# Gate tiles in pairs: sums of the seven products made in open PSUM banks, copied out by ScalarE

## The chip, the cores and the metric

The kernel runs on one core of a Trainium2 chip. A core has TensorE (PE, the matrix multiplier, with its weight loads PEld beside it), VectorE (DVE), ScalarE (ACT), GpSimd (POOL) and SyncE (SP, which issues nearly all DMA transfers here). Each engine has a queue of its own, worked off in order, and engines wait for one another through semaphores. PE writes its products into PSUM, eight banks of 128 x 512 float32 each, which DVE and ACT read; everything else lies in SBUF or in device memory. The metric is the time of one execution in microseconds (us) on the device.

## The reference

A decoder layer with two attention branches for one sequence of 2048 tokens, width 1024. One input projection gives the queries, keys and values of both branches, and the gates:

```python
xn = rms_norm(h, norm_gain[l])
proj = xn @ w_in[l]
sb_q, sb_k, sb_v, sw_q, sw_k, sw_v, sb_z, sw_z, g_sb, g_sw = jnp.split(proj, offsets, axis=-1)
...
y_sb = (o_sb * jax.nn.silu(sb_z)) @ w_branch_sb[l]
y_sw = (o_sw * jax.nn.silu(sw_z)) @ w_branch_swa[l]
merged = jax.nn.sigmoid(g_sb) * y_sb + jax.nn.sigmoid(g_sw) * y_sw
h = h + merged @ w_out[l]
```

The change concerns columns of this projection that become gates: `sb_z` and `sw_z` go through SiLU (a value times its sigmoid), `g_sb` and `g_sw` through a sigmoid.

## The kernel before

The tokens are cut into four groups of 512; groups 2 and 3 are worked on first, then 0 and 1. Columns of the projection are cut into tiles of 128. The normalized input is kept transposed as two parts, a rounded high part `xh[g]` and the rest `xl[g]`, and so are the weights (`wh`, `wl`); a product is three matmuls (high x high, high x low, low x high) for each of eight slices of 128 rows. A plain column tile (`col_tile`) is 24 matmuls of 128x512 and its gate is made by `gate` (L1339, L1341).

**Seven products in place of eight.** `gate_pairs` takes two column tiles c and d and the two groups ga and gb of a half at once, as a 2 x 2 block product: the weights are the blocks a11, a12 (tile c) and a21, a22 (tile d), the inputs b11, b21 (group ga) and b12, b22 (group gb), each block four slices deep. Strassen's scheme in Winograd's form makes the four results from seven products. It needs sums of weight blocks, s1 to s4, made for each pair by `pair_weights` (DVE makes the sums r1 to r4, ACT rounds them to high parts `sh`, DVE makes the low parts `sl`), and sums of input blocks, t1 to t4, made once for a call. It runs twice: for the last 16 gate tiles of the first half (eight pairs, 0 to 7), and for eight SiLU tiles of the second half (four pairs, 8 to 11). Pairs 1 to 6 and 8 to 11 are SiLU gates, pairs 0 and 7 are plain sigmoids.

**The work of a pair before.** `product(a, b)` (L1924 to L1932) takes the next of three bank tags g, z, t (two banks each, so six products may be in flight) and runs 12 matmuls, L1929 to L1931. The order is a11·b11, a12·b21, s2·t2, s4·b22, a22·t4, s1·t1, s3·t3. ACT copies the first out of PSUM (L1953); seven additions on DVE (`add`, L1935), each with one operand in PSUM, form the results; `gate_out` applies sigmoid (L1940, L1943) and for SiLU a multiplication (L1941), and sends the result out by DMA.

**Buffers.** The results and r1 to r4 come from the ring `tmp` of nine tiles of 128x512 (L1112), the s blocks from rings of four (`SB = 4`), the whole weights from rings of three, raw weights from two. A tile is given out in the program's order when an older one is released.

**What sets the order.** PE's order is the order of the program throughout (`manual_schedule`). DVE follows the program up to `ordered()` in the first pair of a call (`byhand.close` or `rest`); ACT follows it up to the call. Otherwise a planner lays out ACT, DVE and SP ahead of time: it simulates the engines, and gives each engine the earliest instruction of the program that is ready in that simulation. On the chip the engines then keep that order, ready or not. Around the calls: in pair 0, `put` (L1740, L1741) still fills t1 and t3; `along` runs squares of the next half's rows (L1892) on ACT in the first call and weight sums for the last projection on DVE in the second; in the last pair of the first call `between` prepares the next group.

Of the kernel before, what the change touches and what calls it, by code (L numbers as in the profile page):

```python
# [10 lines left out]
AF = mybir.ActivationFunctionType  # L11
ALU = mybir.AluOpType
# [37 lines left out]
def tile_kernel(ctx, tc, x, xt, meta, metat, gain, w_in, w_sb, w_sw, w_out, sinks, fgain,  # L50
# [16 lines left out]
    def ps(tag):  # L67
        return pp.tile([P, 512], F32, tag=tag, name="ps_" + tag, bufs={"g": 2, "z": 2, "t": 2, "o": 2}[tag])
# [102 lines left out]
    def drain(*gens):  # L171
        for _ in chain(*gens):
            pass
# [938 lines left out]
    def tmp(dt=F32, rows=P):  # L1112
        return tp.tile([rows, GT], dt, tag="tmp", name="tmp", bufs=9)
# [623 lines left out]
    HK = KT // 2  # L1737
# [114 lines left out]
    def pair_weights(c, d, pool, out, begin=False):  # L1852

        raws, whole = [], []
        for c0 in (c, d):
            raws.append(load(c0))
            whole.append(weights(c0, raw=raws[-1]))
            yield
        a11, a12, a21, a22 = (r[:, j:j + HK, :] for r in raws for j in (0, HK))
        r1, r2, r3, r4 = (tmp().rearrange("p (k c) -> p k c", k=HK) for _ in range(4))  # L1860
        s2, s1, s3, s4 = ([pool.tile([P, HK, P], F32R, tag="s" + i, name="s" + i, bufs=SB) for i in "hl"] for _ in range(4))
        V.tensor_tensor(r1, a21, a22, op=ALU.add)
        V.tensor_tensor(r2, r1, a11, op=ALU.subtract)
        if begin:
            A.copy(s2[0], r2)
            A.copy(s1[0], r1)
        V.tensor_tensor(r3, a11, a21, op=ALU.subtract)
        if begin:
            A.copy(s3[0], r3)
            V.tensor_tensor(s2[1], r2, f32(s2[0]), op=ALU.subtract)  # L1870
            yield
        V.tensor_tensor(r4, a12, r2, op=ALU.subtract)
        if begin:
            A.copy(s4[0], r4)
        for (h, l), r in ((s2, r2), (s1, r1), (s3, r3), (s4, r4)):
            if not begin:
                A.copy(h, r)
            if r is not r2 or not begin:
                V.tensor_tensor(l, r, f32(h), op=ALU.subtract)
        (h1, l1), (h2, l2) = whole  # L1880
        out.extend([(h1[:, :HK, :], l1[:, :HK, :]), (h1[:, HK:, :], l1[:, HK:, :]), (h2[:, HK:, :], l2[:, HK:, :]),
                    s1, s2, s3, s4])
# [34 lines left out]
    def gate_pairs(ga, gb, pairs, pool, sums_x, nxt, ordered, along, between):  # L1917

        t1, t2, t3, t4 = sums_x[:4]
        b11, b21 = ((xh[ga][:, j:j + HK, :], xl[ga][:, j:j + HK, :]) for j in (0, HK))  # L1920
        b22 = xh[gb][:, HK:, :], xl[gb][:, HK:, :]

        banks = iter(range(1 << 30))

        def product(a, b):
            acc = ps("gzt"[next(banks) % 3])
            (wh, wl), (h, l) = a, b
            for k in range(HK):
                T.matmul(acc, lhsT=wh[:, k, :], rhs=h[:, k, :], start=k == 0, stop=False)  # L1929
                T.matmul(acc, lhsT=wh[:, k, :], rhs=l[:, k, :], start=False, stop=False)  # L1930
                T.matmul(acc, lhsT=wl[:, k, :], rhs=h[:, k, :], start=False, stop=k == HK - 1)  # L1931
            return acc  # L1932

        def add(t, acc, u):
            V.tensor_tensor(t, acc, u, op=ALU.add)  # L1935

        def gate_out(dst, t, silu):
            if silu:
                e = tmp()
                A.activation(e, t, AF.Sigmoid)  # L1940
                V.tensor_tensor(t, t, e, op=ALU.mult)  # L1941
            else:
                A.activation(t, t, AF.Sigmoid)  # L1943
            DMA(dst, t)

        for n, ((_, cdst, csilu), (_, ddst, dsilu)) in enumerate(pairs):
            a11, a12, a22, s1, s2, s3, s4 = nxt
            end = n + 1 == len(pairs)
            if n and not end:
                nxt = []  # L1950
                drain(pair_weights(pairs[n + 1][0][0], pairs[n + 1][1][0], pool, nxt))
            p, u, v, w = (tmp() for _ in range(4))
            A.copy(p, product(a11, b11))  # L1953
            more = product(a12, b21)
            add(u, product(s2, t2), p)
            add(p, more, p)
            if not n:
                nxt = []
                ordered()
                drain(pair_weights(pairs[1][0][0], pairs[1][1][0], pool, nxt))  # L1960
            gate_out(cdst[ga], p, csilu)
            next(along, None)
            if end:
                between()
            p3 = product(s4, b22)
            p4 = product(a22, t4)
            p5 = product(s1, t1)
            add(v, p5, u)
            add(v, p3, v)
            gate_out(cdst[gb], v, csilu)  # L1970
            add(u, product(s3, t3), u)
            add(w, p5, u)
            gate_out(ddst[gb], w, dsilu)
            add(u, p4, u)
            gate_out(ddst[ga], u, dsilu)


    sbt = [lambda p=p, f=f: f(p) for f, p in ((sb_k, 0), (sb_k, 1), (sb_q, 0), (sb_v, 0), (sb_v, 1), (sb_q, 1),
# [174 lines left out]
    for half, groups in enumerate(halves):  # L2153
        gts = [lambda spec=spec: gate(*spec) for spec in specs[half]]
        if half == 1:
            with tc.tile_pool(name="fast1", bufs=1, side="left") as bp:
                byhand, hand = ExitStack(), ExitStack()
                byhand.enter_context(tc.manual_schedule(engines={mybir.EngineType.DVE}))
                hand.enter_context(tc.manual_schedule(engines={mybir.EngineType.Activation}))
                vsplit[0] = True  # L2160
                ts = [mk() for mk in sbt[:3]]
                *sums_x, late_lows, side = combined_anew(*groups, rs1, bp, short)
                pairs = list(zip(swz[::2], swz[1::2]))
                nxt = []
# [88 lines left out]
        if half == 0:  # L2253
            with tc.tile_pool(name="fast", bufs=1, side="left") as bp:
# [25 lines left out]
        else:  # L2280
# [95 lines left out]
```

## Time and profile before

| | |
|---|---|
| time, median of 3 runs | 2049.21 us (2048.4 to 2049.78) |
| span of the profiled execution, first to last instruction | 2045.8 us |
| its own time | not listed apart from the span; the median is 3.4 us above it |
| first call of `gate_pairs` | 580.4 to 733.9 us of the span |
| second call | 777.6 to 854.1 us |

The profile is one execution recorded by the hardware profiler. Its page gives the busy time of each engine, the chain of work that ended last, and groups of instructions by source line. The trace behind it answers further views: windows (busy time of each engine in a stretch), waits (who waited for whom), and a timeline, whose rows are start, duration, engine, source line, operation, output<-inputs, shapes and count; brackets hold the idle time ahead of an instruction and what ended it. Consecutive instructions of one kind may be merged in a row ("x3"). Matmuls overlap: a matmul's row is longer than the step from one to the next.

### The profile page before, as it was taken

Reading aid. Unit: us, or ns where it says so; the run is one execution under the profiler, and the core shown is the slowest. Engines: PE = TensorE matmul, PEld = TensorE weight load, DVE = VectorE, ACT = ScalarE, POOL = GpSimd, SP = SyncE. Lnnn points to the kernel's source line nnn. Section 1 sums busy time; section 2 is a strip of 40 time slices with the busy share of each in tenths; the row PEclk is TensorE's granted clock in tenths of the full one; section 3 lists DMA queues with packets and bytes.
Section 4 is the critical chain, followed back from the end, with each engine's and each line's share of the span. In section 5 each row is a group of like instructions: output and inputs, shape, how many; then the busy total and the mean of one; then the engine's idle time right before and its main releaser. Section 6 shows DMA issues by size and latency. Waiting matters only on the chain.

```text
span 2045.8 us, 31245 instructions
## 1 busy us (share of the span) xinstructions
PE 2031.7 (99%) x10375; PEld 1706.3 (83%) x10375; DVE 1649.3 (81%) x2708; ACT 1177.5 (58%) x2825; POOL 311.4 (15%) x642
## 2 busy tenths in 40 slices
PE   9999999999999999999999999999999999999998
PEld 7888888888888888888888888888888888887887
DVE  7898986877788789658887389999997788788788
ACT  6677775576755343358777366667766442335234
POOL 1233444431000000003333101000000003000000
PEclk9999999999999999999999999999999999999999
DMA  9855554865468669844344554344323779886942
GB/s 336 321 197 199 179 200 165 260 194 170 135 233 306 228 214 315 309 147 162 132 178 150 173 156 116 115 127 126 109 83 105 266 257 313 290 284 200 307 150 98
DMA packets 184065, 409.32 MB, mean 200 GB/s; under 512 B 25280, under 2 KB 29760, under 8 KB 183904
## 3 DMA queue, kind: packets, MB, share of 16 engines
q1 hardware_dynamic: 183616, 407.06, 59.0%
q8 instruction: 82, 1.34, 0.3%
q14 instruction: 79, 0.65, 0.1%
q10 hardware_dynamic: 288, 0.27, 0.0%
HBM read 256.36 MB, written 148.32 MB: 198 GB/s over the span
## 4 chain that ended last, share of the span: by engine, by line
PE 95%; ACT 2%; DVE 2%; DMA 1%; issue 1%; POOL 0%; SPq 0%; ACTq 0%; DVEq 0%; POOLq 0%
PE ps_g L1188 35%; PE ps_o L1700 6%; PE ps_z L1643 6%; PE ps_t L1668 6%; PE ps_z L1188 3%; PE ps_z L1484 3%; PE ps_o L1540 2%; PE ps_t L1518 1%; PE ps_g L1929 1%; PE ps_g L1930 1%; PE ps_g L1931 1%; PE ps_o L338 1%; PE ps_o L337 1%; PE ps_o L339 1%; PE ps_z L1929 1%; PE ps_z L1930 1%
## 5 line engine op out<-in xcount | busy, mean ns | idle before, releaser
L1188 PE MATMUL ps_g<-xh,wh 128*128 128x512 f32 x1088 | 442.3, 406 | 0.1
L1188 PE MATMUL ps_g<-xl,wh 128*128 128x512 f32 x1088 | 426.2, 392 | 0.7 <-DVE xl L2001 0.6
L1188 PE MATMUL ps_g<-xh,wl 128*128 128x512 f32 x1088 | 425.7, 391 | 0.0
L1653 DVE TENSOR_TENSOR_SCAN row<-row 128x512 f32<-128x512 f32 (+4 forms) x256 | 288.6, 1128 | 47.6 <-POOL row L1648 30.7
L1188 PEld LDWEIGHTS ps_g<-xh,wl 128*128 128x128 f32 x1088 | 204.2, 188 | 45.5 <-DVE wl L2049 0.4
L1646 ACT ACTIVATE row<-ps_z 128x512 f32<-128x512 f32 (+4 forms) x352 | 175.1, 509 | 110.3 <-PE ps_z L1643 106.3
L1188 PEld LDWEIGHTS ps_g<-xl,wh 128*128 128x128 f32 x1088 | 205.3, 189 | 34.5 <-DVE xl L2001 2.0
L1188 PEld LDWEIGHTS ps_g<-xh,wh 128*128 128x128 f32 x1088 | 204.9, 188 | 34.1 <-ACT xh L2000 0.6
L128 DVE SCALAR_TENSOR_TENSOR wtl<-ps_t,wth 128x512 fp32r<-128x512 f32 (+1 forms) x320 | 188.2, 588 | 11.3 <-ACT wth L127 11.1
L127 ACT ACTIVATE wth<-ps_t 128x512 fp32r<-128x512 f32 (+1 forms) x320 | 171.6, 536 | 41.9 <-PE ps_t L1668 39.4
L1643 PE MATMUL ps_z<-kt,q 128*128 128x512 f32 (+4 forms) x704 | 184.1, 350 | 0.7 <-ACT row L1646 0.7
L1668 PE MATMUL ps_t<-ident,row 128*128 128x128 f32 x1088 | 172.3, 273 | 1.8 <-DVE wtl L128 1.6
L1668 PEld LDWEIGHTS ps_t<-ident,row 128*128 128x128 f32 x1088 | 133.1, 140 | 35.7 <-DVE wtl L128 5.8
L1643 PEld LDWEIGHTS ps_z<-kt,q 128*128 128x128 f32 x704 | 123.8, 188 | 24.1 <-ACT row L1646 3.1
L1700 PE MATMUL ps_o<-wth,vc 128*128 128x512 f32 (+1 forms) x320 | 134.9, 422 | 0.0
L1492 ACT ACTIVATE sc<-sc,nm 128x129 f32<-128x129 f32 x256 | 100.0, 393 | 30.3 <-DVE nm L1490 29.2
L1700 PE MATMUL ps_o<-wtl,vc 128*128 128x512 f32 (+1 forms) x320 | 116.6, 364 | 0.2 <-DVE wtl L128 0.2
L1659 POOL COPY mr<-row 128x16 f32<-128x16 f32 x128 | 33.3, 263 | 382.3 <-DVE row L1653 347.7
L1477 POOL COPY sc<-skb 128x4 f32<-128x4 f32 x64 | 16.0, 256 | 458.0 <-PE ps_g L1931 304.0
L1339 ACT ACTIVATE tmp<-ps_g 128x512 f32<-128x512 f32 x63 | 37.8, 599 | 78.7 <-PE ps_g L1188 72.7
L1651 DVE TENSOR_TENSOR_SCAN row<-row,mask 128x512 f32<-128x512 f32 (+2 forms) x64 | 69.6, 1093 | 16.1 <-ACT row L1646 16.0
L1524 POOL TENSOR_SCALAR_AFFINE_SELECT pm<-ph 64x256 fp32r<-64x256 f32 x128 | 62.2, 486 | 114.7 <-ACT ph L127 110.5
(926 smaller groups left out, 4684.3 us busy)
## 6 DMA issues: line engine op xcount, KB each, us to landing
wh<-h_in_w_in SPq DMA_DIRECT2D x66, 512.0 KB, 4.0
wl<-l_in_w_in SPq DMA_DIRECT2D x66, 512.0 KB, 5.3
raw<-in_w_in SPq DMA_DIRECT2D x57, 512.0 KB, 5.6
h_in_w_in<-wh SPq DMA_DIRECT2D x50, 512.0 KB, 3.1
l_in_w_in<-wl SPq DMA_DIRECT2D x50, 512.0 KB, 4.2
q<-qd SPq DMA_DIRECT2D x128, 128.0 KB, 3.1
vc<-vd SPq DMA_DIRECT2D x48, 256.0 KB, 3.1
kd<-tmp SPq DMA_DIRECT2D x32, 256.0 KB, 3.2
```

The costliest lines, as they stand in the source:

```text
L127: A.activation(h, acc, AF.Copy, scale=scale)
L128: V.scalar_tensor_tensor(l, acc, scale, f32(h), op0=ALU.mult, op1=ALU.subtract)
L1188: T.matmul(acc, lhsT=a[:, k, :], rhs=b[:, k, :], start=k == i == 0, stop=k == KT - 1 and i == 2)
L1484: T.matmul(acc[:, a * 256:(a + 1) * 256], lhsT=lq, rhs=kk[:, 2 * kv + hl, blk * P:(blk + 2) * P], start=hl == 0, stop=hl == 1)
L1492: A.activation(sc[:, hh, :], sc[:, hh, :], AF.Exp, bias=nm[:, hh:hh + 1], accum_out=den[:, hh:hh + 1])
L1524: G.affine_select(out=pm[to, :, c], in_=full[r, :, c], pattern=[[0, 4], [sign, HB]], compare_op=ALU.is_ge, fill=0.0, base=n - 1, channel_m ...
L1643: T.matmul(z[:, :m], lhsT=qt[:, j * P:(j + 1) * P], rhs=kt[h][:, k0 + c:k0 + c + m], start=t == 0, stop=t == 1)
L1646: A.activation(r[:, c:c + m], z[:, :m], AF.Sigmoid, scale=-1.0)
L1651: V.tensor_tensor_scan(r[:, :w], r[:, :w], mask[:, :w], 1.0, op0=ALU.mult, op1=ALU.max)
L1653: V.tensor_tensor_scan(r[:, :w], r[:, :w], r[:, :w], last[j] if n else 1.0, op0=ALU.mult, op1=ALU.min)
L1668: T.transpose(tr[:, j * P:(j + 1) * P], rows_of[h, g, n - (j > i), j][:, k0:k0 + P], ident)
L1700: T.matmul(o[:, :n], lhsT=v, rhs=r, start=first and r is wh, stop=last)
```

## The change

The product order of a pair becomes a11·b11, a12·b21, s2·t2, s1·t1, s3·t3, s4·b22, a22·t4. `product` now writes into a bank that it is given and may leave it open, so that a later product adds onto it. One bank (`chain_of`) collects a11·b11, s2·t2, s3·t3 and a22·t4 in turn; a second (`two`) s1·t1 and s4·b22; a third (`other`) holds a12·b21. In between ACT copies the open banks' sums to SBUF: after the first, third and fifth product from `chain_of`, after the fourth from `two`. DVE adds three times a pair: p (the c result of ga), w (d of gb) and u (c of gb). The d result of ga is complete in `chain_of`, and its gate reads PSUM directly. Copies take their `tmp` tile when they are made; before, all four were taken at the head of the pair.

```diff
-        def product(a, b):
-            acc = ps("gzt"[next(banks) % 3])
+        def product(acc, a, b, start=False, stop=False):
             (wh, wl), (h, l) = a, b
             for k in range(HK):
-                T.matmul(acc, lhsT=wh[:, k, :], rhs=h[:, k, :], start=k == 0, stop=False)
...
+                T.matmul(acc, lhsT=wh[:, k, :], rhs=h[:, k, :], start=start and k == 0, stop=False, skip_group_check=True)
...
-        def add(t, acc, u):
-            V.tensor_tensor(t, acc, u, op=ALU.add)
-
-        def gate_out(dst, t, silu):
+        def copied(acc):
+            t = tmp()
+            A.copy(t, acc)
+            return t
+
+        def gate_out(dst, t, silu, src=None):
             if silu:
                 e = tmp()
-                A.activation(e, t, AF.Sigmoid)
-                V.tensor_tensor(t, t, e, op=ALU.mult)
+                A.activation(e, t if src is None else src, AF.Sigmoid)
+                V.tensor_tensor(t, t if src is None else src, e, op=ALU.mult)
             else:
-                A.activation(t, t, AF.Sigmoid)
+                A.activation(t, t if src is None else src, AF.Sigmoid)
             DMA(dst, t)
...
-            p, u, v, w = (tmp() for _ in range(4))
-            A.copy(p, product(a11, b11))
-            more = product(a12, b21)
-            add(u, product(s2, t2), p)
-            add(p, more, p)
+            chain_of, other, two = ps("g"), ps("z"), ps("t")
+            product(chain_of, a11, b11, True)
+            p = copied(chain_of)
+            product(other, a12, b21, True, True)
+            product(chain_of, s2, t2)
+            u = copied(chain_of)
+            V.tensor_tensor(p, other, p, op=ALU.add)
...
-            p3 = product(s4, b22)
-            p4 = product(a22, t4)
-            p5 = product(s1, t1)
-            add(v, p5, u)
-            add(v, p3, v)
-            gate_out(cdst[gb], v, csilu)
-            add(u, product(s3, t3), u)
-            add(w, p5, u)
+            product(two, s1, t1, True)
+            w = copied(two)
+            product(chain_of, s3, t3)
+            v = copied(chain_of)
+            product(two, s4, b22, stop=True)
+            V.tensor_tensor(w, w, v, op=ALU.add)
             gate_out(ddst[gb], w, dsilu)
-            add(u, p4, u)
-            gate_out(ddst[ga], u, dsilu)
+            V.tensor_tensor(u, two, u, op=ALU.add)
+            gate_out(cdst[gb], u, csilu)
+            product(chain_of, a22, t4, stop=True)
+            gate_out(ddst[ga], v, dsilu, chain_of)
```

More of the change, by code (lines that the diff above doesn't have):

```diff
@@ L1921, in gate_pairs @@
         b22 = xh[gb][:, HK:, :], xl[gb][:, HK:, :]
-        banks = iter(range(1 << 30))
-        def product(a, b):
-            acc = ps("gzt"[next(banks) % 3])
+        def product(acc, a, b, start=False, stop=False):
             (wh, wl), (h, l) = a, b
             for k in range(HK):
[L1929 to L1932, printed above, removed]
-        def add(t, acc, u):
-            V.tensor_tensor(t, acc, u, op=ALU.add)
-        def gate_out(dst, t, silu):
+                T.matmul(acc, lhsT=wh[:, k, :], rhs=h[:, k, :], start=start and k == 0, stop=False, skip_group_check=True)
+                T.matmul(acc, lhsT=wh[:, k, :], rhs=l[:, k, :], start=False, stop=False, skip_group_check=True)
+                T.matmul(acc, lhsT=wl[:, k, :], rhs=h[:, k, :], start=False, stop=stop and k == HK - 1, skip_group_check=True)
+        def copied(acc):
[3 more added lines that the diff above has]
+        def gate_out(dst, t, silu, src=None):
             if silu:
                 e = tmp()
-                A.activation(e, t, AF.Sigmoid)
-                V.tensor_tensor(t, t, e, op=ALU.mult)
+                A.activation(e, t if src is None else src, AF.Sigmoid)
+                V.tensor_tensor(t, t if src is None else src, e, op=ALU.mult)
             else:
-                A.activation(t, t, AF.Sigmoid)
+                A.activation(t, t if src is None else src, AF.Sigmoid)
             DMA(dst, t)
```

## The prediction

> **What bounds the kernel now.** First the page: the busy times, then the chain of work that ended last.
>
> ```profile
> PE 2031.7 (99%) x10375; PEld 1706.3 (83%) x10375; DVE 1649.3 (81%) x2708; ACT 1177.5 (58%) x2825; POOL 311.4 (15%) x642
> ...
> PE 95%; ACT 2%; DVE 2%; DMA 1%; issue 1%; POOL 0%; SPq 0%; ACTq 0%; DVEq 0%; POOLq 0%
> ```
>
> TensorE (PE) is busy 99% of the span and 95% of the chain is its own. That is a mean over stages, so the windows view was cut to the two calls of `gate_pairs` (eight pairs, then four), and to the second pair of the first call.
>
> ```profile
> core 0 of [0], span 2045.8 us
> core 0: us, PE busy (x) PEld busy (x) DVE busy (x) ACT busy (x) POOL busy (x), PEclk, DMA share, GB/s
> 580.40:733.90 153.50, 153.49 (x679) 126.57 (x678) 121.62 (x188) 78.75 (x138) 0.00 (x0) 1.00 0.73 268
> 777.60:854.10 76.50, 76.50 (x339) 63.37 (x338) 59.55 (x96) 21.52 (x37) 0.00 (x0) 1.00 0.93 333
> 599.50:618.90 19.40, 19.39 (x86) 15.60 (x85) 15.88 (x25) 14.71 (x33) 0.00 (x0) 1.00 0.99 357
> ```
>
> In both calls PE is busy for all of the time. VectorE (DVE), which the change relieves, has 121.62 of 153.50 us: much, but not all. A busy PE may still hide short gaps, so next comes the view of PE's waits; its first and last of nine rows are these.
>
> ```profile
> PE ps_t L1668 <- DVE wtl L128: 1.6, 5, 0.5
> ...
> PE ps_o L1700 <- DVE wtl L128: 0.2, 1, 0.2
> ```
>
> The nine add up to 6.2 us for the whole kernel, and none of them names L1929 to L1931, the matmuls of `product`. **There is no stall in this stage that the change could remove.** The unit of the stage comes from PE's timeline in pair 0 (pairs are counted 0 to 7 in the first call, 8 to 11 in the second).
>
> ```profile
> 583.38 0.39 PE L1929 MATMUL ps_z<-xh,wh 128*128 128x512 f32 x1
> ...
> 586.10 0.39 PE L1929 MATMUL ps_t<-t2h,sh 128*128 128x512 f32 x1
> ```
>
> The second product begins at 583.38 and the third at 586.10: 2.72 us for 12 matmuls, one each 0.227 us. A matmul's row is 0.39 long, so a product ends 0.16 us after the next has begun.
>
> **What is removed, added and moved.** *PE*: seven products of 12 matmuls a pair, before and after. Nothing is saved there.
>
> *DVE*: seven additions become three. One lasts this long:
>
> ```profile
> L1935 DVE TENSOR_TENSOR tmp<-ps_t,tmp 128x512 f32<-128x512 f32 x18 | 12.3, 686 | 5.2 <-PE ps_t L1931 5.0
> ```
>
> 4 x 12 x 0.686 = 33 us of DVE work go. All of it lies beside PE, which doesn't wait for it: worth nothing on the path. Where a delay goes, PE's next matmul is "late next", and it is already back to back.
>
> *ScalarE (ACT)*: three more copies a pair, 36 in all, at 0.58 us (rows below): 21 us. In pair 1 ACT would go from 14.71 to 16.5 of 19.4 us. This too lies beside PE, unless PE waits for a copy.
>
> *The new wait.* This is what decides. Before, each product had a bank of its own out of six, so nobody cared when one was read. Now `chain_of` and `two` stay open and are copied in the middle: PE may not go on in the bank until ACT has read it, and PE's order is written by hand, so all matmuls behind the waiting one wait too. Each pair has four such places: the copy of p must be done before s2·t2 (third product), u before s3·t3 (fifth), w before s4·b22 (sixth), v before a22·t4 (seventh). Exactly one other product lies in between, so the time allowed is 2.72 - 0.16 = 2.56 us, of which the copy itself takes 0.58: ACT may come 1.98 us late.
>
> How late does ACT come? The copy of p exists before the change (L1953). In pair 0:
>
> ```profile
> 586.62 0.59 ACT L1339 ACTIVATE tmp<-ps_g 128x512 f32<-128x512 f32 x1
> 587.11 1.65 ACT L1740 CAST xh<-xs 128x512 fp32r<-128x512 f32 x3
> 588.66 0.58 ACT L1953 COPY tmp<-ps_g 128x512 f32<-128x512 f32 x1
> ```
>
> It ends at 589.24, while s2·t2 began at 586.10. In front of it stand a gate of the last plain tile and three casts of `put`, which come earlier in the program and which the change leaves alone; the planner has no new reason to place the copy sooner. **Pair 0: 589.24 - 586.10 = +3.1 us.** The same happens where the second call begins (PE's row, then ACT's):
>
> ```profile
> 783.24 0.39 PE L1929 MATMUL ps_t<-t2h,sh 128*128 128x512 f32 x1
> ```
>
> ```profile
> 784.05 0.62 ACT L1874 CAST sh<-tmp 128x512 fp32r<-128x512 f32 x1 [1.47 <-DVE tmp L1872]
> 784.57 0.59 ACT L1339 ACTIVATE tmp<-ps_z 128x512 f32<-128x512 f32 x1
> 785.06 0.58 ACT L1953 COPY tmp<-ps_g 128x512 f32<-128x512 f32 x1
> ```
>
> **Pair 8: 785.64 - 783.24 = +2.4 us.** In pairs 1, 2, 4 and 9 the rows are these, the third product's begin and then the copies, in the same order.
>
> ```profile
> 605.14 0.42 PE L1929 MATMUL ps_g<-t2h,sh 128*128 128x512 f32 x1
> ...
> 624.55 0.39 PE L1929 MATMUL ps_z<-t2h,sh 128*128 128x512 f32 x1
> ...
> 662.63 0.39 PE L1929 MATMUL ps_g<-t2h,sh 128*128 128x512 f32 x1
> ...
> 802.28 0.39 PE L1929 MATMUL ps_g<-t2h,sh 128*128 128x512 f32 x1
> ```
>
> ```profile
> 614.74 0.58 ACT L1953 COPY tmp<-ps_z 128x512 f32<-128x512 f32 x1
> ...
> 630.19 0.58 ACT L1953 COPY tmp<-ps_t 128x512 f32<-128x512 f32 x1
> ...
> 663.56 0.58 ACT L1953 COPY tmp<-ps_z 128x512 f32<-128x512 f32 x1
> ...
> 807.40 0.58 ACT L1953 COPY tmp<-ps_z 128x512 f32<-128x512 f32 x1
> ```
>
> At their old places the copies would hold PE for 10.2, 6.2, 1.5 and 5.7 us. But here lateness was free, and its reason is one that the change itself weakens. A pair takes 12 or so tiles from the ring `tmp` of nine: r1 to r4 of the next pair's weights, then p, u, v, w and a scratch tile for each SiLU. The r tiles are asked for first, and p waits for a slot. Two things now free slots sooner: the s products stand third to sixth instead of third, fourth, sixth and seventh, so the casts that need the old s buffers, and with them r3 and r4, are done one product (2.7 us) sooner; and the gates come after the fifth, sixth and seventh product, where before three came after the sixth and seventh. Counted through with the SiLU scratch, when p is wanted the slots hold u, w, v, one scratch, four r and p: exactly nine. So in the steady pairs 3 to 6, 10 and 11 I take 0 (bounds 0 and 1.5 each for 3 to 6, from pair 4). Pairs 1 and 2 are crowded besides (ACT 14.71 of 19.4 us, DMA at 0.99), with squares and weight casts that may stand ahead of a copy: 2.5 us together, between 0 and 16.4, near the low end because the slots come back. Pair 9: 0.6, between 0 and 5.7. The other 36 copies have no row: between 0 and, if a weight cast (1.05), an s cast (0.62) and a sigmoid of about that length stand ahead, 2.3 - 1.98 = 0.3 each, 11 in all; the cast alone fits, so I take 0.5.
>
> *What is moved.* s1·t1 and s3·t3 come two products sooner, s4·b22 and a22·t4 two later. In pair 0 t1 and t3 are still being made then:
>
> ```profile
> 590.32 1.89 DVE L1741 TENSOR_TENSOR xl<-xs,xh 128x512 fp32r<-128x512 f32 x3
> 592.12 2.35 DVE L120 TENSOR_TENSOR wl<-raw,wh 128x1024 fp32r<-128x1024 f32 x2
> 594.40 0.69 DVE L1741 TENSOR_TENSOR xl<-xs,xh 128x512 fp32r<-128x512 f32 x1
> 595.00 1.89 DVE L1741 TENSOR_TENSOR t3l<-tt,t3h 128x512 fp32r<-128x512 f32 x3
> ```
>
> Delayed by 3.1, s1·t1 begins at 586.10 + 3.14 + 2.72 = 591.96 and wants its last xl ten matmuls later, at 594.2; DVE has it at 595.09: +0.8. s3·t3 then begins at about 595.5, with t3l coming from 595.6 on, one each 0.6 us against 0.68 that PE needs: +0.1. The DMAs of a pair are as many and as large as before, 2 gate results for each of two groups; w and u enter SP's queue sooner and no load is moved behind a longer wait, so I cost them at 0. If DMA at 0.99 delays a raw tile, the weight cast that waits for it holds up the copy behind it on ACT; that is inside the bounds of pairs 1 and 2.
>
> **Sum**: 3.1 + 0.8 + 0.1 (pair 0) + 2.5 (pairs 1, 2) + 2.4 (pair 8) + 0.6 (pair 9) + 0.5 = 10.0 us. The profiled execution's span goes from 2045.8 to 2055.8; the median of 2049.21 stands 3.4 us above that span (start and end lie around it), so the forecast is 2049.2 + 10 = **2059 us**.
>
> **The rivals.** *Copies in time (not slower).* The planner orders ACT by its simulated time, and a pair's stall shifts the rest of that order. If the copies of pairs 0 and 8 go ahead of the casts and slots suffice elsewhere, what is left is under 4 us: 2049 to 2053. It decides at one point: pair 0's copy must start before 585.5 (586.10 - 0.58). Against it: the four ACT rows ahead of 588.66 are the same instructions after the change. For it: ACT was idle for 1.47 us ahead of 784.05 with the first product of pair 8 done. Chance 0.20.
>
> *All old lateness becomes stall (much slower).* If the ring still makes p wait, the places cost 3.1 + 10.2 + 6.2 + 4 x 1.5 + 2.4 + 5.7 = 33.6 us, and 2049.2 + 33.6 = 2083. For it: the rows as they stand. Against it: the slot count above. From the rows, a product at half the clock would cost 2.72 us more, and stalls of 10.2 and 6.2 us are the ones that could bring that about: two such, 2088. The clock in every window of this trace is 1.00, and no line of PE waits for more than 1.6 us in all, so the trace has no case of it. The Trainium skill's page "TensorE: Matmul & The Clock Gate" (Part 1: The HAM clock gate) says that an idle time of about 3.4 us halves the clock until some 3.4 us of work have passed; no run here shows it yet, and by that rule pair 0's stall stays just under the limit. Chance 0.13.
>
> *Faster.* Only if all but 2 of the 6.2 us of PE's waits went, by another order of ACT and DVE in later stages: 2043 to 2045. Nothing in the change aims there. Chance 0.05.
>
> **How the numbers follow.** The forecast (4 to 20 us more, 2053 to 2069) has 0.62. A measurement of this kernel can tell about 0.2%, 4 us, from no change. Slower: 0.62 + 0.13 = 0.75; within: 0.20; faster: 0.05. The range leaves out the lower half of the rival "in time", the faster case and the top of the "all lateness" case: 2051 to 2077.
>
> **What would show it.** Right: PE rows of `product` waiting for ACT's copy line in the waits view, about 3 us in pair 0 and 2 in pair 8; DVE additions x36; ACT copies x48; PE's busy time unchanged, span longer by the sum of those waits. Wrong: no such wait (then the planner moved the copies), or waits of over 5 us in pairs 1 and 2 (then the ring still binds), or a granted clock under 1.00 behind a stall. A change of PE's time in the attention stages would speak for the planner, not for these steps.

## The result, and the profile after

The changed kernel takes 2064.97 us (median of 4 runs, 2063.23 to 2067.52), the kernel before beside it 2048.9 (2048.4 to 2049.78). The ratio is 1.0083, with a 95% interval of 1.0071 to 1.0096: **0.8% slower, 16 us**. The span of the profiled execution goes from 2045.8 to 2061.5 us.

First the busy times on the page of the changed kernel, then the windows view of the two calls of `gate_pairs`.

```profile
span 2061.5 us, 31254 instructions
...
PE 2035.1 (99%) x10375; PEld 1708.4 (83%) x10375; DVE 1621.9 (79%) x2660; ACT 1195.2 (58%) x2861; POOL 312.3 (15%) x642
```

```profile
580.40:742.20 161.80, 154.22 (x680) 126.46 (x679) 105.73 (x159) 91.98 (x164) 0.00 (x0) 1.00 0.72 253
786.00:868.60 82.60, 78.53 (x339) 64.17 (x338) 54.19 (x87) 28.79 (x52) 0.00 (x0) 0.98 0.85 302
```

PE has the same 10375 matmuls. DVE has 48 instructions fewer, and they bought nothing: PE, which was busy for all of both calls, is now idle for 7.6 us of the first and 4.1 us of the second, and the second call's granted clock is 0.98. The waits view of PE, columns as before, names the new wait in its first two rows:

```profile
PE ps_g L1926 <- ACT tmp L1932: 7.8, 3, 4.0
PE ps_t L1926 <- ACT tmp L1932: 3.3, 1, 3.3
...
PE ps_t L1927 <- DVE xl L1741: 0.5, 1, 0.5
```

L1926 is a matmul of `product`, L1932 the copy out of an open bank. PE's timeline gives the places; the bracket is the idle time ahead.

```profile
589.30 0.47 PE L1926 MATMUL ps_g<-t2h,sh 128*128 128x512 f32 x1 [3.12 <-ACT tmp L1932]
...
595.05 0.50 PE L1927 MATMUL ps_t<-xl,sh 128*128 128x512 f32 x1 [0.50 <-DVE xl L1741]
...
596.46 0.50 PE L1926 MATMUL ps_g<-t3h,sh 128*128 128x512 f32 x1 [0.67 <-ACT tmp L1932]
...
602.77 0.50 PE L1926 MATMUL ps_t<-xh,sh 128*128 128x512 f32 x1 [3.29 <-ACT tmp L1932]
```

```profile
795.69 0.62 PE L1926 MATMUL ps_g<-t2h,sh 128*128 128x512 f32 x1 [4.02 <-ACT tmp L1932]
```

All of it lies in the first pair of each call. In pair 0, s2·t2 waits for the copy of p, s1·t1 for its last `xl`, s3·t3 for the copy of u, s4·b22 for that of w; in pair 8, s2·t2 for the copy of p. Taken from step to step (the time from one matmul's begin to the next, less the usual 0.227), the waits are 3.28, 0.66, 0.84 and 3.45 us, and 4.18 in pair 8. Pairs 1 to 7 and 9 to 11 have none.

In pair 8 something is added. Two windows of the same execution, one ending with the wait and the next:

```profile
792.50:795.92 3.42, 0.23 (x1) 0.23 (x2) 3.42 (x7) 1.67 (x4) 0.00 (x0) 1.00 0.86 293
795.92:799.33 3.41, 3.41 (x9) 2.63 (x9) 3.41 (x6) 0.00 (x0) 0.00 (x0) 0.50 0.97 366
```

For 3.41 us behind the wait the granted clock is 0.50, and 9 matmuls run where 15 would.

The account closes. Measured from the first to the last matmul of `product`, the first call takes 161.27 us against 152.93 before, the second 82.23 against 75.93. The first call's 8.3 us are its waits (8.23). The second's 6.3 are 4.18 of waiting, 1.7 of slow clock (most of the nine steps behind the wait take 0.427 us in place of 0.227) and 0.4 of short delays, of which 0.2 are a wait for the copy of w in pair 8. The other 1.1 us of the span lie behind the second call, and I did not follow them.

### The profile page after: what moved, and what is told of

Same layout as the page of the kernel before. It is cut to its first block, busy times and chain, and to the rows that moved or that the text cites. A ratio compares the mean times of both kernels' runs of the same rounds, so it can differ in the third digit from the quotient of the medians.

```text
span 2061.5 us, 31254 instructions
## 1 busy us (share of the span) xinstructions
PE 2035.1 (99%) x10375; PEld 1708.4 (83%) x10375; DVE 1621.9 (79%) x2660; ACT 1195.2 (58%) x2861; POOL 312.3 (15%) x642
## 4 chain that ended last, share of the span: by engine, by line
PE 83%; DVE 7%; DMA 4%; ACT 3%; issue 1%; POOL 0%; SPq 0%; DVEq 0%; ACTq 0%
PE ps_g L1188 33%; PE ps_o L1700 6%; PE ps_z L1643 6%; PE ps_t L1668 6%; PE ps_z L1484 3%; PE ps_o L1540 2%; PE ps_g L1926 2%; PE ps_g L1928 2%; PE ps_g L1927 2%; PE ps_t L1518 1%; PE ps_o L338 1%; PE ps_o L337 1%; PE ps_o L339 1%; PE ps_z L1188 1%; PE ps_t L1926 1%
```

## The experiments

In the table, "call 1" and "call 2" are the two calls, by how much they are longer than in the kernel before, in us (first to last matmul of `product`, from each version's trace), with the sum of those waits of PE in them that are over 0.4 us and the time at half clock, in which a part of a wait may lie. One trace was taken of each.

| version | median, us | ratio and interval | call 1 (waits; half clock) | call 2 (waits; half clock) |
|---|---|---|---|---|
| the change | 2064.97 | 1.0083 [1.0071, 1.0096] | +8.3 (8.2; 0) | +6.3 (4.2; 3.4) |
| e1 first pairs as before, three bank tags | 2064.95 | 1.0082 [1.0067, 1.0097] | +10.3 (7.5; 6.8) | +5.8 (3.6; 3.4) |
| e2 own tiles for the first pairs' copies | 2064.72 | 1.0085 [1.0068, 1.0102] | +9.8 (8.6; 3.4) | +6.4 (3.6; 6.8) |
| e3 the new order alone | 2059.0 | 1.0053 [1.0038, 1.0068] | +3.8 (3.9; 0) | +6.0 (4.5; 3.4) |
| e4 first pairs' copies with priority | 2061.99 (one run) | | +7.9 (6.3; 3.4) | +7.9 (4.9; 6.8) |
| e5 as e1, more bank tags | 2068.64 | 1.0098 [1.0084, 1.0111] | +11.0 (9.4; 10.2) | +6.6 (5.7; 0) |
| e6 five crowded pairs as before | 2052.29 | 1.0020 [1.0011, 1.0029] | +1.3 (1.6; 0) | +3.9 (3.5; 0) |
| e8 own tiles, s1·t1 sixth | 2062.95 | 1.0069 [1.0052, 1.0086] | +13.7 (10.4; 10.2) | +1.9 (1.6; 0) |
| e9 s1·t1 sixth alone | 2065.32 | 1.0082 [1.0067, 1.0097] | +7.3 (5.0; 3.4) | +7.8 (5.0; 6.8) |
| e10 pair 1's weights later | 2067.32 | 1.0092 [1.0077, 1.0107] | +12.4 (7.9; 10.2) | +7.1 (4.5; 6.8) |
| e11 own tiles, old order | 2060.05 | 1.0056 [1.0039, 1.0073] | +11.0 (9.1; 6.8) | +2.3 (1.9; 0) |
| e12 as e11, pair 1 with own tiles too | 2058.05 | 1.0050 [1.0036, 1.0063] | +6.7 (4.8; 3.4) | +4.0 (3.3; 0) |

The theories at the start: (A) the copies come late because other work of ACT stands ahead of them (the prediction's reason); (B) they come late because the ring `tmp` has no slot for them; (C) the new order asks for operands that are not made yet.

### The first pairs as before (e1)

```diff
+            old = n == 0                       # pairs 0 and 8
+            if old:
+                p, u, v, w = (tmp() for _ in range(4))
+                A.copy(p, closed(a11, b11))    # closed: a bank of its own, tags g, z, t in turn
+                more = closed(a12, b21)
+                add(u, closed(s2, t2), p)
...
```

> The first pair of each call (0 and 8) is made as before the change, with seven closed banks in the old order; the other ten pairs keep the open banks. Theory (all of the loss lies in the first pairs of the two calls, where PE waits for ACT's copies): the 15 us vanish, time of before within 1 us, about 2049; ten pairs run without a stall, and the DVE work that they save (about 27 us) brings nothing. Rival (the loss is spread, by the planner's other order in later stages): still over 2053.

It missed: the time is that of the change. The stalls of pairs 0 and 8 went, but for 1.6 us in pair 8 for weight sums, and the next pairs got others: 5.62 us in pair 1, 2.03 in pair 9. PE's row for pair 1 and then DVE's, from the version's timeline:

```profile
605.66 0.80 PE L1926 MATMUL ps_g<-xh,wh 128*128 128x512 f32 x1 [5.46 <-DVE tmp L1938]
```

```profile
604.92 1.28 DVE L1938 TENSOR_TENSOR tmp<-ps_g,tmp 128x512 f32<-128x512 f32 x2
```

L1938 is here the old pair's addition. Of seven closed products three use tag g, which has two banks; pair 1 opens a fourth g bank, and an addition of pair 0 still has to read the one before the last. The join of the two forms has a wait of its own.

### The join with more bank tags (e5)

```diff
-            acc = ps("gzt"[next(banks) % 3])
+            acc = ps("gztozot"[next(banks) % 7])
```

> As e1 (first pair of each call closed and in the old order), but four of its seven banks are taken elsewhere: products four and six go to the two banks of tag o, idle in this stage, so that the banks that the next pair opens were read long ago. Theory (e1 lost 5.6 and 2.0 us plus slow clock because the next pair opened a bank that a late addition had still to read): both waits ahead of the first product of pairs 1 and 9 vanish; pair 0 and pair 8 run without a stall. Then the copy of p in pair 1, which came 10 us too late before the change and which the stalls of pair 0 have covered so far, may hold PE: 2049 if the ring has slots by then, up to 2059 if not. Rival (the first pairs are not the place of the loss): 2062 or more.

The wait for the addition is gone, but pair 1 now waits 9.36 us for the copy of its p, with the clock at half for 10.2 us. Before the change that copy ended 10.2 us after s2·t2 had begun (the prediction's rows for pair 1): this is that lateness, turned into a wait. In the changed kernel pair 0's stalls had come ahead of it. The second call is no better off: pair 9 waits 1.5 us and pair 10 2.7 for copies.

### Copies first, without a slot and with one (e4, e2)

```diff
+            with tc.high_priority():      # e4, in pairs 0 and 8
                 t = tmp()
                 A.copy(t, acc)
```

> Open banks everywhere; the copies of the first pair of each call, with the taking of their tiles, get the highest priority with the planner. Rival theory (ACT's earlier work goes ahead of the copy by priority): the first copy of pair 0 moves ahead of the casts of xh, the first wait of 3.3 us goes, and that of pair 8: about 2058. Ring theory: a copy without a slot can't go whatever its priority; no change, 2063 to 2067.

```diff
+            if n == 0 and len(pairs) == 8:             # e2: pair 0
+                t = pool.tile([P, GT], F32, tag="first", name="first", bufs=4)
+            elif n == 0 and not spare_rb:              # pair 8, the copy of p
+                t = tp.tile([P, GT], F32, tag="rb", name="spare", bufs=1)
+                spare_rb.append(t)
+            else:
                 t = tmp()
```

> Open banks everywhere, but the copies of pair 0 and the first copy of pair 8 get tiles of their own in place of slots of the ring of nine. Ring theory (a copy comes late since it waits for a slot): the waits ahead of the third product vanish in both pairs; pair 8 loses nothing any more (6.5 us less, slow clock included), pair 0 keeps a wait for xl in the fourth product that the first wait had hidden, 5 to 7 us instead of 8.5: about 2056 to 2058. Rival (ACT's earlier work of the program stands ahead of the copy, as the prediction had it): the copies stay where they are, about 2065.

Priority alone changed little: p is waited for 3.29 us in pair 0 and 4.86 in pair 8, where its rival theory had wanted both waits gone. (The one run took 2061.99 us, 1 us under what the ring theory had said.) A tile of its own brought the copy of pair 0's p forward. ACT's timeline in e2, then in the changed kernel:

```profile
583.66 0.59 ACT L1940 COPY first<-ps_g 128x512 f32<-128x512 f32 x1 [2.09 <-PE ps_g L1928]
584.20 0.62 ACT L1865 CAST sh<-tmp 128x512 fp32r<-128x512 f32 x1
```

```profile
586.01 0.62 ACT L1874 CAST sh<-tmp 128x512 fp32r<-128x512 f32 x1 [0.32 <-DVE tmp L1872]
586.54 0.59 ACT L1339 ACTIVATE tmp<-ps_g 128x512 f32<-128x512 f32 x1
587.03 1.64 ACT L1740 CAST xh<-xs 128x512 fp32r<-128x512 f32 x3
588.58 0.58 ACT L1932 COPY tmp<-ps_g 128x512 f32<-128x512 f32 x1
```

With its own tile the copy follows at once on the product's last matmul (L1928), at 583.66; with a tile of the ring it stands behind the same gate and casts as before the change, at 588.58. **A falls as the reason for p, and B holds**: the planner gave the copy that late place because it had no slot sooner. But the time is the same, 2064.72 us, where the ring theory had 2056 to 2058. PE runs on for one product more and then waits for s1·t1's operand:

```profile
593.04 0.50 PE L1927 MATMUL ps_t<-xl,sh 128*128 128x512 f32 x1 [3.75 <-DVE xl L1741]
```

In pair 8 it is `t1l`, with 3.64 us. C was hidden behind B.

In pair 0 something else is added to C. In e2 DVE makes sums of pair 1's weights (L1862, L1863, L1867), the first of them after a wait for its load, ahead of the last `xl`; in the changed kernel they stand behind it. DVE's timeline in e2, then in the changed kernel:

```profile
591.09 0.69 DVE L1862 TENSOR_TENSOR tmp<-raw 128x512 f32<-128x512 f32 x1 [1.33 <-DMA raw<-in_w_in]
...
597.58 0.69 DVE L1741 TENSOR_TENSOR xl<-xs,xh 128x512 fp32r<-128x512 f32 x1
```

```profile
594.31 0.68 DVE L1741 TENSOR_TENSOR xl<-xs,xh 128x512 fp32r<-128x512 f32 x1
...
597.93 0.68 DVE L1862 TENSOR_TENSOR tmp<-raw 128x512 f32<-128x512 f32 x1
```

The last `xl` comes 3.3 us later. The four versions with tiles of their own in pair 0 (e2, e8, e11, e12) have this order on DVE, and neither the kernel before nor any other version has it. These sums take slots of the ring, so the likely reason is that the copies left theirs free; no run tests that by itself.

### The order alone (e3, e9)

```diff
-            p3 = product(s4, b22)          # e3: before's kernel, closed banks
-            p4 = product(a22, t4)
             p5 = product(s1, t1)
...
             add(u, product(s3, t3), u)
...
+            add(v, product(s4, b22), v)
+            add(u, product(a22, t4), u)
```

> The kernel before, with seven closed banks and seven additions, but with the new order of the products. Theory (t1 and t3 of pair 0 are made too late for the new order): PE waits in pair 0 for xl in the fourth product and perhaps for t3l in the fifth, 4 to 5 us, nothing in the other pairs: about 2053.5. Rival (the order costs nothing by itself): 2049, and the waits for xl in the changed kernel came from its stalls.

With every bank closed and seven additions, the order of the products alone costs 11 us (ratio 1.0053), of which 9.8 lie in the two calls: in the first call PE waits 2.01 and 1.89 us for `xl`, in the second 4.46 for `t1l`, with 3.4 us of half clock. In the second call that is nearly as much as the whole change costs (6.0 against 6.3). The expectation had the waits for `xl` right and missed those for `t1l`.

```diff
+            x = ps("o")                    # e9, pairs 0 and 8
+            product(x, s4, b22, True, True)
             product(chain_of, s3, t3)
             v = copied(chain_of)
+            product(two, s1, t1, True, True)
```

> The same order in pairs 0 and 8, without the tiles of their own. If p's copy waits for a slot whatever comes behind it, the waits ahead of s2*t2 stay at about 3.3 us (pair 0) and 4.2 us (pair 8, with some 2 us for the slow clock), while the waits for xl and for w's copy go (0.7 + 0.8 + 3.5 us): 2049 + 10 = 2059 us (2056 to 2062). The rival, that the order frees the slot sooner too, wants p's waits under 2 us and 2054 or less.

The waits came as expected where they were (3.28 us for p in pair 0; 4.95 in pair 8, somewhat longer), and those for `xl` and for w went. The time didn't come: pair 1 has 1.67 us, and the clock fell to half behind both stalls, for 3.4 and 6.8 us.

### Both at once (e8, e11)

```diff
+            x = ps("o")                    # e8 = e2 and e9 together
...
+            p3, p4 = ps("o"), ps("z")      # e11 = e2 with before's order of all seven
+            product(p3, s4, b22, True, True)
+            product(p4, a22, t4, True, True)
+            product(two, s1, t1, True, True)
...
+            product(chain_of, s3, t3, stop=True)
```

> Pairs 0 and 8 keep the open bank of p, u and v, but their copies have tiles of their own, and s1*t1 goes back to the sixth place (s4*b22 closed in a fourth bank, one addition more); the other ten pairs are as in the changed kernel. If two causes together make up the loss, a slot of the ring that comes late for p's copy and operands of s1*t1 that come late for its new place, then neither pair has a wait of over 1 us, the clock stays at full rate, and what is left is the 1.7 and 0.9 us that the version with own tiles alone had in pair 1: 2049 + 3 = 2052 us (2049 to 2056). The rival, that the lateness of a stage's first pairs has to show somewhere, wants a wait of 3 us or more in pair 1 or 9 and 2058 to 2065.

> Pairs 0 and 8 run the seven products in the order of the kernel before, with p, u and v still copied out of one open bank, their copies in tiles of their own (one in pair 8, for p), and five additions; the other ten pairs are as in the changed kernel. s3*t3 is the last product again, so t3l, which held up the version before by 5.2 us, has its old time. If a late slot and operands that the new order wants too early are the whole loss, no wait of over 1 us is left in pair 0 or 8, the clock stays at full rate, and some 1 to 3 us of waits in pairs 1 and 9 remain: 2049 + 2.5 = 2051.5 us (2049 to 2055). The rival, that the lateness of a stage's first pair is passed on to pair 1's copies, as with closed banks there, wants a wait of 3 us or more in pair 1 and 2057 or more.

In the second call this settles the greater part. Neither cause removed: +6.3 us. Own tile alone: +6.4. Old place of s1·t1 alone: +7.8. Both: +1.9 (e8), +2.3 (e11) and, with the same second call, +4.0 (e12, below), each with the clock at full rate. **Two causes stand one behind the other, and taking away either leaves a wait for the other.** What is left are 1.4 to 1.6 us in pair 8 for its weight sums and up to 1.7 in pair 9 for the copy of p.

In the first call both versions missed. In e8 s3·t3 stands in fifth place, and PE waited 1.8 us for `t3h` and 5.2 for `t3l`, which DVE makes last: I had moved only one of the two products whose operands come late, and with the tiles of their own pair 1's weight sums stand ahead of `t3l`, as in e2. (In e9, which has the same order of products without these tiles, PE waits for neither, though there p's stall of 3.28 us gives them time.) In e11 nothing but 1.75 us for `xl` is left in pair 0, where DVE waits 1.37 us for the load of those weights and makes three of their sums ahead of the last `xl`; and pair 1 has this:

```profile
613.80 0.80 PE L1926 MATMUL ps_g<-t2h,sh 128*128 128x512 f32 x1 [7.14 <-ACT tmp L1940]
```

The rival of that expectation was right: the lateness is passed on to pair 1's copies.

### Is it the ring again in pair 1? (e10, e12)

```diff
-                drain(pair_weights(pairs[1][0][0], pairs[1][1][0], pool, nxt))
...
             v = copied(chain_of)           # e10
+            if not n:
+                drain(pair_weights(pairs[1][0][0], pairs[1][1][0], pool, nxt))
```

> The changed kernel, with the making of pair 1's weights called behind the copy of v in pair 0 and not ahead of its gate. The theory that w's copy in pair 0 comes late because squares and casts stand ahead of it on ScalarE wants the wait of 3.45 us ahead of s4*b22 to go, and nothing else to change: 2065 - 3.5 = 2061.5 us, less if pair 0's slow clock goes too. The rival, that w's copy also waits for a slot of the ring, wants a wait of 2 us or more at the same place and 2064 or more; that pair 1's weights then come late would show as waits for sh or sl in pair 1.

The wait for w in pair 0 fell from 3.45 to 0.6 us, so what held that copy were the weights of pair 1, made earlier in the program. In the changed kernel ACT's timeline shows this:

```profile
600.48 0.63 ACT L1892 ACTIVATE xs<-xs 128x512 f32<-128x512 f32 x1 [0.72 <-DMA xs<-in_x]
601.02 0.19 ACT L1892 ACTIVATION_READ_ACCUMULATOR xs<-xs 128x1 f32 x1
601.11 1.12 ACT L1877 CAST sh<-tmp 128x512 fp32r<-128x512 f32 x2
602.14 0.57 ACT L1932 COPY tmp<-ps_t 128x512 f32<-128x512 f32 x1
```

The copy of w, before which s4·b22 could not begin at 599.3, stands behind a square that waits for its load and two casts of those weights. Whether the casts hold it or the ring's slots that their sums take, e10 does not tell, since it moves both. The theory thus had the wait right and the time wrong: 4.0 us appeared ahead of pair 1's s2·t2, the clock was at half for 10.2 us of the first call, and the median is 2067.32 us.

```diff
-            if n == 0 and len(pairs) == 8:
-                t = pool.tile([P, GT], F32, tag="first", name="first", bufs=4)
+            if n < 2 and len(pairs) == 8:
+                t = pool.tile([P, GT], F32, tag="first", name="first", bufs=8)
```

> The version before, with tiles of its own for the copies of pair 1 too (eight in all, so that pairs 0 and 1 take no slot of the ring for them); nothing else is changed. With them the copy of pair 1's p stands ten instructions earlier in ScalarE's order: behind the cast that waited for its load until 605.27 us and two squares, in place of six squares, two casts and three sigmoids. If the ring's slots are what passes the lateness on from pair to pair, the wait of 7.3 us ahead of pair 1's s2*t2 shrinks to what that cast and the squares leave (605.3 + 1.0 + 1.6 + 0.6 = 608.5, against 606.3: some 2.2 us), the clock stays at full rate, and the time is 2060 - 5 - 3 = 2052 us (2049 to 2055). The rival, that ScalarE as a whole is late because its casts and squares wait for loads, wants 4 us or more of waits in pairs 1 and 2 still, at other copies or products, and 2055 to 2061.

Pair 1's wait fell from 7.30 to 0.59 us, so it was the slot that held its copy. The clock fell to half all the same, because pair 2, whose copies use the ring, now waits 2.16 us for its p. The waits of the first call went down from 9.1 to 4.8 us, no lower, and the median of 2058.05 lies where the rival has it, though pairs 1 and 2 have 2.75 us between them and not 4. Whether pair 2's copy of p waits for a slot was not tested: on ACT it stands behind a weight cast that waits 1.10 us for PE, and a square. The 2.0 us for `xl` in pair 0 are again DVE's weight sums ahead of it, with 1.63 us of waiting for their load.

### The crowded pairs as before (e6)

```diff
+            old = n < (3 if len(pairs) == 8 else 2)      # pairs 0 to 2, 8 and 9 closed
```

> Closed banks and the old order in the five crowded pairs (0 to 2, 8 and 9), with the banks of e5, open banks in the other seven. Theory (open banks cost nothing where ring and ACT have room; DVE's saving brings nothing): no wait of PE on the lines of product, time of before within 0.1%. Rival one (DVE's time was worth something): faster than before by over 2 us. Rival two (open banks cost by themselves, or later stages are laid out worse): over 2052.

This is the only version near the kernel before: 2052.29 us against 2048.72, a ratio of 1.0020 [1.0011, 1.0029]. Seven of the twelve pairs still have open banks. The theory, which wanted no wait and the old time within 0.1%, missed; 2052.29 is just over the bound of rival two, by too little to tell. What is left are waits at the joins, 1.56 us in pair 3 and 2.32 in pair 10 for the copy of p, and 1.1 us in pair 8 for its weight sums (`sh`, `sl`). So the open banks cost nothing where ACT and DVE keep up, as pairs 4 to 7 and 11 show here and pairs 1 to 7 and 9 to 11 in the changed kernel, and they cost where these run late. No version was faster than the kernel before: what DVE saves bought nothing in any of them.

### Stalls of chosen length (e7)

```diff
                 v = copied(chain_of)
+                if len(pairs) == 8:
+                    for _ in range({3: 8, 4: 10, 5: 12, 6: 14}.get(n, 0)):
+                        A.copy(v, chain_of)
```

> As e6, and in pairs 3, 4, 5 and 6 the copy of v is repeated 8, 10, 12 and 14 times more, so that PE waits for ACT by about 2, 3, 4 and 5 us ahead of its seventh product. Theory (a stall of about 4 us makes the clock fall to half for 3.4 us, a stall of 3 us mostly doesn't): matmuls follow one another at 0.43 us instead of 0.23 behind the longer two stalls, granted clock 0.5 for 3.4 us each, 1.6 us lost beside each stall itself; nothing behind the shorter two. Rival (the slow stretches of the changed kernel came from something else): 0.23 us behind all four.

PE waited 3.74, 4.98, 6.22 and 7.45 us in pairs 3 to 6, about 2 us more than was meant, and the clock then was at half for 3.4, 6.8, 6.8 and 6.8 us. So the stalls of 2 and 3 us, for which the theory had said that the clock mostly holds, were not made in these pairs. The four waits are 22.4 us, the kernel is 33.7 us slower than e6 (2086.02, one run). The rival, full rate behind all four, fell. What decides is seen when the windows are cut where the clock changes, 3.41 us each:

```profile
653.91:657.32 3.41, 2.20 (x10) 1.50 (x8) 1.82 (x3) 3.28 (x7) 0.00 (x0) 1.00 0.16 61
657.32:660.73 3.41, 1.04 (x5) 0.86 (x6) 0.81 (x2) 2.56 (x5) 0.00 (x0) 1.00 0.00 0
660.74:664.15 3.41, 3.41 (x10) 2.67 (x9) 1.90 (x3) 1.03 (x3) 0.00 (x0) 0.50 0.42 154
...
855.29:858.71 3.42, 1.65 (x8) 1.05 (x7) 2.77 (x5) 0.59 (x1) 0.00 (x0) 1.00 1.01 362
858.71:862.12 3.41, 3.41 (x10) 2.66 (x9) 2.88 (x5) 0.03 (x1) 0.00 (x0) 0.50 1.01 371
```

The stall of 3.74 us fell across two windows; the second was idle enough, and the window after it ran at 0.50. The last two rows are a wait of only 1.94 us, in pair 10: it lay inside one window, and the next ran at half.

## Why the prediction was right, and where it was wrong

**What bounds the kernel: right.** PE was the bound, DVE's saving bought nothing, and the change is slower by waits of PE for copies out of open banks. The time lies inside the range, 6 us above the forecast. Term by term:

- *Copy of p, pair 0: 3.1, measured 3.28.* The size was right, and its reason was wrong. The prediction put it down to ACT's work ahead, for which "the planner has no new reason to place the copy sooner". e2 shows that the planner places it 4.9 us sooner (583.66 against 588.58) as soon as it has a tile: the ring's slot held it. The prediction had the ring in its account, but counted slots for the steady pairs only.
- *Copy of p, pair 8: 2.4, measured 4.18.* The mechanism was right, the size was off. The copy came 10.0 us later than before the change (795.06 against 785.06), and the product that wants it 8.3 us later (791.51 against 783.24); the 1.7 us more enter at a load between the calls, as DVE's rows before and after the change show:

```profile
740.37 0.75 DVE L1155 SCALAR_TENSOR_TENSOR tt<-tt,gn 128x512 f32<-128x512 f32 x1 [1.95 <-DMA tt<-in_xt]
```

```profile
750.91 1.42 DVE L1155 SCALAR_TENSOR_TENSOR tt<-tt,gn 128x512 f32<-128x512 f32 x2 [5.19 <-DMA tt<-in_xt]
```

SP issued that load at 744.40 against 733.90, 10.5 us later. From there to pair 8 DVE and ACT run about 10.0 us later than before, PE 8.3. What held the load in SP's queue stays open.

- *The other 36 copies: 0.5, measured 4.5*: in pair 0 0.84 for u and 3.45 for w, in pair 8 0.2 for w. This is the term that was mis-sized most. The bound of 0.3 each was worked out from one weight cast, one s cast and one sigmoid ahead of a copy. The rows above have a square that waits for its load in that queue, and e10 shows that the weights of pair 1, made in that place, delay w, by their work or by their slots.
- *s1·t1's `xl`: 0.8, measured 0.66; s3·t3: 0.1, measured nothing of its own.* These held, but only behind the stall of p. e3 and e2 show what the new order costs without that cover: 3.9 and 6.1 us for `xl` in pair 0 (in e2 with the weight sums that DVE makes ahead of it), and 4.5 and 3.6 for `t1l` in pair 8. For pair 8 the prediction had not looked at `t1l` at all.
- *Pairs 1, 2 and 9: 2.5 and 0.6, measured 0.* Not because their copies had ceased to be late, as the slot count argued. In e5 and e11, which take most of pair 0's stalls away, pair 1 waits 9.4 and 7.3 us. Where pair 0 waits longer, pair 1 mostly waits less: 8.2 and 0 us in the changed kernel, 6.3 and 0 in e4, 6.1 and 2.5 in e2, 3.9 and 4.0 in e10 (e9, with 3.3 and 1.7, is out of line). The reading that fits is that ACT and DVE catch up while PE waits.
- *The clock: 0 in the sum, measured 1.7 us* behind pair 8's stall. It stood only in the rival with long stalls, and a granted clock under 1.00 behind a stall was one of the prediction's own signs of being wrong. That the clock is 1.00 in every window of the trace before holds for the windows shown; at that trace's end, behind a window without a matmul (2039.80 to 2043.21 us), it is 0.50. The Trainium skill's page "TensorE: Matmul & The Clock Gate" (Part 1: The HAM clock gate) was weighed there as "no run here shows it yet"; the changed kernel and nearly every version here show it.

Together: the first call 6.5 (3.1 + 0.8 + 0.1 + 2.5) against 8.3, the second 3.0 against 6.3, with 0.5 for other copies in either, and nothing against 1.1 in the stages behind. That the forecast came within 6 us is in part luck: 3.1 us for pairs 1, 2 and 9 that did not come stand against 4.0 too little for the other copies, 1.8 for p in pair 8, 1.7 for the clock and 1.1 behind the calls.

**The rivals.** "All old lateness becomes stall" was right on one point, that lateness which cost nothing before is paid by PE now, and wrong on the sum. The places do not add up: 33.6 us of lateness became 12.4 us of waits, and where one pair waits the next waits less. Ten of the eleven versions in the table have between 3.9 and 10.4 us of waits in the first call, whichever cause is removed; only e6, which gives the first three pairs their closed banks again, has 1.6. "Copies in time" was wrong: p's copy started at 588.58 and not before 585.5.

**Open.** What the first call would cost if pairs 0 to 2 all had tiles of their own, or with a longer ring, for which there is no run; why the second call keeps waits of 1.6 to 3.3 us with both causes removed; and whether the loads (DMA at 0.99 in pair 1 before the change) are behind ACT's lateness. Some of ACT's waits are for them, but no run takes the loads away.

## What to carry to other kernels

Where the bound engine is busy throughout, work taken from another engine is worth nothing, and buffers between the two may be worth much: before giving up a bank that is read late for free, look up in the trace how late its reader comes, in the crowded pairs and not in the steady ones. When a wait is removed and the time stays, look for the next wait in the same place before rejecting the cause: in the second call here a buffer slot and an operand's due time stood one behind the other, and only removing both brought time back. Look also at what moves into the room that a change makes: in the versions with tiles of their own, other sums went ahead of an operand that PE wanted. A stall also changes how late everything behind it is, so the latenesses of one trace are not added up.

## What the runs showed of the hardware

The granted clock is decided in fixed windows. In each trace all stretches at half clock begin at times that differ by whole multiples of 3.413 us: in e7 at 660.74, 684.63, 711.94, 739.24 and 858.71, which are 7, 8, 8 and 35 windows apart. What counts is how much of such a window PE was idle, not how long the stall was. Over the thirteen traces with stalls, each full-rate window inside the two calls in which PE was idle for 2.06 us or more was followed by one at half clock, and none with 2.04 or less. Nearest to that edge are the window of e7 above that begins at 855.29 (2.06 us idle) and one of the changed kernel (2.04). Two windows, each with the one after it: the first pair is from e12 (2.08 us idle), the second is that of the changed kernel.

```profile
628.53:631.95 3.42, 1.46 (x6) 1.24 (x7) 2.76 (x6) 3.39 (x6) 0.00 (x0) 1.00 1.04 416
631.95:635.36 3.41, 3.41 (x9) 2.64 (x8) 1.01 (x5) 2.48 (x5) 0.00 (x0) 0.50 1.04 414
```

```profile
597.94:601.36 3.42, 1.53 (x7) 0.94 (x5) 2.56 (x5) 2.70 (x8) 0.00 (x0) 1.00 1.06 401
601.36:604.77 3.41, 2.00 (x9) 1.67 (x10) 2.59 (x4) 3.41 (x9) 0.00 (x0) 1.00 0.94 326
```

(The idle times are worked out from matmul begins at 0.227 us each; the busy column is a little longer, since a matmul's row is 0.39 us.) So a stall of 2.1 us can cost the clock if it falls into one window, as 1.94 us with a short gap beside it did in e7; one of 3.28 in pair 0 cost it in e4, e9 and e10 and not in the changed kernel, where it fell across two windows; and a stall of over some 4.1 us, twice that edge, can't stay under it in both of two windows (all twelve such stalls here cost the clock). The loss is 1.6 to 1.7 us for a slow window full of work (1.7 in the changed kernel's second call, 1.6 in e12's first, as sums of the steps' excess over 0.227 us). The Trainium skill's page "TensorE: Matmul & The Clock Gate" (Part 1: The HAM clock gate) gives the window, 3413 ns, and says that it runs free; the traces agree. It gives an idle window, about 3.4 us, as the limit; here 2.06 us of one were enough.
